# Second norm of a transformer layer: GpSimd's product moved to VectorE, and the order of the work around it

## The chip, the cores and the metric

The kernel runs on one core of a Trainium2 chip. The metric is the device time of one execution in microseconds (us), the median of several runs. The engines are TensorE (PE in the rows, with its weight loads as PEld), VectorE (DVE), ScalarE (ACT), GpSimd (POOL) and SyncE (SP), which issues most of the transfers.

## The reference, cut to what matters

One layer handles 512 prompt and 32 sample positions (544 columns) of 1024 features. All of it is fp32. The change lies between the layer's first residual sum and its FFN:

```
x  = x + gate1 * (merged @ w_out)
h2 = RMSNorm(x) * g_norm2 * (1 + scale2) + shift2      # RMSNorm: x * rsqrt(mean(x*x) + eps) over the features
up, gate = split(h2 @ w_up)
x  = x + gate2 * ((silu(dwconv3_causal(up)) * gate) @ w_down)
```

The scale, shift and gate come from a conditioning vector, one value for each feature and stream (prompt or sample). A final RMSNorm follows.

## The kernel before

Features lie on the 128 partitions (8 groups k = 0 to 7 of 128 features), positions on the free axis. The 544 columns are two halves of 272: 256 prompt and 16 sample columns each. Since scale and shift differ by stream, an operation that uses them is issued twice for a half, on 256 and on 16 columns (`streams`).

Every fp32 matrix product is made of three products of a high and a low part: `mm3_steps` issues for each k the matmuls (weight high, x high), (weight high, x low) and (weight low, x high), 272 columns each. So x must be split too: ScalarE writes the high part (a copy that rounds, L91), VectorE the low part (value less high part, L92).

Around the second norm the work stands as follows.

- `out_half(i)` computes the last four of eight output tiles of `merged @ w_out` (m = 4 to 7) for half i alone: 24 matmuls for each m. After each, `residual` adds the tile to x on VectorE (L676, one instruction for each stream), ScalarE squares the new row (L680), and GpSimd adds the squares of m = 1 to 6 into `sacc` (L682). The square of m = 7 stays apart in `sq2`.
- `norm(half)` sums the squares over the partitions with two matmuls against ones (L689, `ssh`; in the trace each has two records), and `rstd_of` makes `rs`, the reciprocal root, with ScalarE (L170, L172) and VectorE (L171, L174 to L176).
- `h2(half)` makes the normalised input for each k: GpSimd multiplies x by `rs` (L699, `hf`), VectorE applies scale and shift (L702, two instructions), then the split: high part by ScalarE (L91, `h2h`), low part by VectorE (L92, `h2l`).
- `up_half(half)` multiplies by the first three tiles of `w_up` (`first`: up tile 0, gate tile 0, up tile 1), whose weights are loaded and split ahead and which hold all three PSUM accumulators (`acc`).

The calls stand in this order: `out_half(0)`, `out_half(1)`, norm of half 0, `h2` of half 0, norm of half 1, `up_half(0)`, `h2` of half 1, `up_half(1)`. A scheduler then sets the order on each engine, and each engine executes its own list strictly in order. `after(inst, earlier)` tells that scheduler that `inst` stands behind `earlier`. Before, only the scale and shift instructions of k = 5 to 7 of half 0 are put behind the last residual sum of half 1 (`done`).

After `up_half(1)` come the other tiles of the FFN, each with a fresh accumulator. The next product (gate tile 1) takes the accumulator of up tile 0, once ScalarE has copied that tile out of PSUM (L752).

Of the kernel before, what the change touches and what calls it, by code (L numbers as in the profile page):

```python
# [12 lines left out]
F32 = mybir.dt.float32  # L13
F32R = mybir.dt.float32r
AF = mybir.ActivationFunctionType
ALU = mybir.AluOpType
# [34 lines left out]
def build(tc, a):  # L51
    nc = tc.nc
    ctx = ExitStack()
    with ctx:
# [34 lines left out]
        def split(hi, lo, x, eng=nc.vector):  # L89

            nc.scalar.copy(hi, x)  # L91
            eng.tensor_tensor(lo, x, hi.bitcast(F32), ALU.subtract)  # L92
# [10 lines left out]
        HALF = ((0, HT), (HT, T))  # L103

        def mm3_steps(ps, wh, wl, xh, xl, k0=0, nk=KD, first=True, last=True, cols=HALF):
            for k in range(nk):
                for w, xs in ((wh, (xh, xl)), (wl, (xh,))):
                    for n, x in enumerate(xs):
                        s = first and k == 0 and w is wh and n == 0
                        e = last and k == nk - 1 and w is wl  # L110
                        for i, (c0, c1) in enumerate(cols):
                            nc.tensor.matmul(ps[:, i, 0:c1 - c0], w[:, k], x[:, k0 + k, c0:c1], start=s, stop=e)  # L112
                yield

        def mm3(*args, **kw):
            for _ in mm3_steps(*args, **kw):
                pass
# [3 lines left out]
        def acc():  # L121
            acc_pools.rotate(-1)
            return acc_pools[-1].tile([P, 2, 512], F32, tag="mm", name="ps")[:, :, 0:HT]
# [30 lines left out]
        def after(inst, earlier):  # L154

            tc.add_manual_dep(inst.ins, earlier.ins.name,
                              mybir.DependencyInfo(mybir.DependencyClass.NoSync, mybir.DependencyReason.DATA))
# [27 lines left out]
        mods = cp.tile([P, 6, KD, 2], F32, name="mods")  # L185
# [144 lines left out]
        for k in range(KD):  # L330
# [5 lines left out]
            hf = xt[:, k]  # L336
# [4 lines left out]
        for w, slot, post in zip(ws, slots, (queries, keys)):  # L341
            ps = slot[:, :, 0:HT]
# [166 lines left out]
        earlier = None  # L509
        for j in range(NP):  # L510
            for e in range(2):
# [7 lines left out]
                earlier = (j, e, transposed(sg), vt)  # L519
# [112 lines left out]
        for b, w0, wb, br in ((0, 7 * KD, "w_branch_b", (bh, bl)), (1, 6 * KD, "w_branch_a", (oh, ol))):  # L632
# [7 lines left out]
            for m in range(KD):  # L640
                ps = proj(W[w0 + m], x)
                sg = mbp.tile([P, 2, HT], F32, tag="sg", bufs=2, name="sgm")
                last = nc.scalar.activation(sg, ps, AF.Sigmoid)
                ps = proj(load_w(a[wb][m], lo=nc.gpsimd), br)
# [15 lines left out]
        xr = xp.tile([P, KD, T], F32, name="xr")  # L660
# [3 lines left out]
        rs = xp.tile([P, T], F32, name="rs")  # L664
        sq2 = xp.tile([P, T], F32, name="sq2")

        def streams(c0, c1):

            e = c0 // HT * HT + HP
            return [(n, a_, b_) for n, a_, b_ in ((0, c0, min(c1, e)), (1, max(c0, e), c1)) if a_ < b_]  # L670

        def residual(ps, s, m, c0, c1):

            for n, a_, b_ in streams(c0, c1):
                r = xr[:, m, a_:b_]
                added = nc.vector.scalar_tensor_tensor(r, ps[:, a_ - c0:b_ - c0], mods[:, s, m, n:n + 1], r,  # L676
                                                       ALU.mult, ALU.add)
            sq = sacc[:, c0:c1] if m == 0 else sq2[:, c0:c1] if m == KD - 1 else \
                xp.tile([P, HT], F32, tag="sq", bufs=2, name="sq")
            nc.scalar.activation(sq, xr[:, m, c0:c1], AF.Square)  # L680
            if 0 < m < KD - 1:
                nc.gpsimd.tensor_tensor(sacc[:, c0:c1], sacc[:, c0:c1], sq, ALU.add)  # L682
            return added
# [8 lines left out]
        h2h = hp.tile([P, KD, T], F32R, tag="hh", name="h2h")  # L692
        h2l = hp.tile([P, KD, T], F32R, tag="hl", name="h2l")

        def h2(c0, c1, earlier=None):

            for k in range(KD):
                hf = xp.tile([P, HT], F32, tag="hf", bufs=6, name="hf2")
                nc.gpsimd.tensor_tensor(hf, xr[:, k, c0:c1], rs[:, c0:c1], ALU.mult)  # L699
                for n, a_, b_ in streams(c0, c1):  # L700
                    v = hf[:, a_ - c0:b_ - c0]
                    v = nc.vector.tensor_scalar(v, v, mods[:, 4, k, n:n + 1], mods[:, 3, k, n:n + 1], ALU.mult, ALU.add)  # L702
                    if earlier and k >= 5:
                        after(v, earlier)
                split(h2h[:, k, c0:c1], h2l[:, k, c0:c1], hf)

        tables = log_tables(last)
        wo = tc.alloc_tile_pool(name="wo", bufs=1)
# [1 line left out]
        for m in range(KD - NW):  # L710
            ps = proj(a["w_out"][m], (mh, ml))
# [2 lines left out]
        late = [(m, load_w(a["w_out"][m], pool=wo, hl_bufs=NW)) for m in range(KD - NW, KD)]  # L714

        def out_half(i):
            for m, w in late:
                ps = acc()[:, 0:1]
                mm3(ps, *w, mh, ml, cols=(HALF[i],))
                done = residual(ps[:, 0], 2, m, *HALF[i])  # L720
            return done

        def up_half(i):
            for w, ps in first.values():
                mm3(ps[:, i:i + 1], *w, h2h, h2l, cols=(HALF[i],))

        out_half(0)
        done = out_half(1)
# [3 lines left out]
        first = {m: (load_w(a["w_up"][m], pool=early, hl_bufs=3), acc()) for m in (0, KF, 1)}  # L732
# [14 lines left out]
        for f in range(KF):  # L747
            ps = first[f][1] if f in first else proj(a["w_up"][f], (h2h, h2l))
# [7 lines left out]
            ps = first[KF][1] if f == 0 else proj(a["w_up"][KF + f], (h2h, h2l))  # L756
# [7 lines left out]
        for m in range(KD - 1):  # L764
            ps = acc()
# [8 lines left out]
        m = KD - 1  # L774
# [7 lines left out]
        for c in HALF:  # L782
            ps = acc()[:, 0:1]
# [3 lines left out]
            cs = slice(*c)  # L787
# [74 lines left out]
```

## Time and profile before

| What | Value |
|---|---|
| Median of 3 runs | 1077.73 us (1075.47 to 1080.16) |
| Profiled execution, its own time | 1078.02 us |
| Span of that execution, first to last instruction | 1075.9 us |
| Busy in the span: TensorE | 1035.5 us (96%) |
| VectorE | 616.3 us (57%) |
| ScalarE | 390.1 us (36%) |
| GpSimd | 159.6 us (15%) |
| Mean granted TensorE clock, as a share of full speed | 0.987 |

The shares are averages over the whole span. The 2.1 us between span and time lie outside the instructions.

### The profile page before, as it was taken

How to read it: one execution, taken by the hardware profiler on the slowest of the kernel's cores; microseconds unless marked ns; L12 is line 12 of the kernel's file. 1: busy time of each engine (PE TensorE's matmuls, PEld its weight loads, DVE VectorE, ACT ScalarE, POOL GpSimd, SP SyncE). 2: the span in 40 equal slices, each digit the busy share in tenths (PEclk: the TensorE clock that was granted, in tenths of full speed). 3: DMA queues.
4: the chain of work that ended last, by engine and by line, in shares of the span. 5: the costliest groups of instructions: out<-in, count | busy, mean ns of one | idle time of the engine just before them, and what ended most of it. 6: DMA issues, size and time to landing. Idle time of an engine off the chain costs nothing.

```text
span 1075.9 us, 19430 instructions
## 1 busy us (share of the span) xinstructions
PE 1035.5 (96%) x8106; PEld 1017.2 (95%) x8106; DVE 616.3 (57%) x930; ACT 390.1 (36%) x655; POOL 159.6 (15%) x245
## 2 busy tenths in 40 slices
PE   2899999999999999999999999999999999999995
PEld 1689999999999999999999999999999999999995
DVE  6956666565675557566667568545455544422234
ACT  5455555444443332121222343333233323322231
POOL 2410010000001111211121135000010001000112
PEclk9799999999999999999999999999999999999998
DMA  9636555454212224555545650022322232332312
GB/s 374 236 88 199 140 143 145 142 140 129 80 50 89 95 83 141 175 179 173 187 166 177 213 203 1 22 98 79 99 79 98 79 98 80 91 87 76 90 53 83
DMA packets 43272, 133.45 MB, mean 124 GB/s; under 512 B 5296, under 2 KB 8496, under 8 KB 43056
## 3 DMA queue, kind: packets, MB, share of 16 engines
q1 hardware_dynamic: 43040, 132.07, 38.5%
q8 instruction: 63, 1.03, 0.4%
q14 instruction: 25, 0.20, 0.1%
q10 hardware_dynamic: 144, 0.14, 0.1%
HBM read 112.60 MB, written 6.75 MB: 111 GB/s over the span
## 4 chain that ended last, share of the span: by engine, by line
PE 92%; DVE 4%; issue 1%; DMA 1%; ACT 1%; POOL 0%; SPq 0%; DVEq 0%; POOLq 0%; ACTq 0%
PE ps L112 83%; PE z L371 2%; PE o L371 2%; PE at L413 2%; DVE hf L702 1%; PE slot L112 1%; PE mt L315 1%; DVE adum L196 1%; DMA cbc<-in_c_dram 1%; DVE h2l L92 1%; DVE xt L337 0%; PE so L371 0%; PE tp L268 0%; SPq L289 0%; POOL hl L92 0%
## 5 line engine op out<-in xcount | busy, mean ns | idle before, releaser
L99 ACT CAST wh<-raw 128x1024 fp32r<-128x1024 f32 x153 | 159.1, 1040 | 362.2 <-PE ps L112 264.3
L100 DVE TENSOR_TENSOR wl<-raw,wh 128x1024 fp32r<-128x1024 f32 (+1 forms) x133 | 162.1, 1221 | 190.2 <-ACT wh L99 189.6
L112 PE MATMUL ps<-hh,wh 128*128 128x272 f32 x992 | 209.3, 291 | 0.0
L112 PE MATMUL ps<-hh,wl 128*128 128x272 f32 x992 | 205.2, 288 | 0.0
L112 PE MATMUL ps<-hl,wh 128*128 128x272 f32 x992 | 204.9, 288 | 0.0
L112 PEld LDWEIGHTS ps<-hh,wh 128*128 128x128 f32 x992 | 156.0, 188 | 1.6 <-issue 0.5
L112 PEld LDWEIGHTS ps<-hl,wh 128*128 128x128 f32 x992 | 155.7, 188 | 0.0
L112 PEld LDWEIGHTS ps<-hh,wl 128*128 128x128 f32 x992 | 155.1, 189 | 0.0
L112 PE MATMUL ps<-h2l,wh 128*128 128x272 f32 x704 | 150.1, 289 | 1.1 <-DVE h2l L92 1.0
L112 PE MATMUL ps<-h2h,wl 128*128 128x272 f32 x704 | 150.6, 290 | 0.0
L112 PE MATMUL ps<-h2h,wh 128*128 128x272 f32 x704 | 150.1, 289 | 0.3 <-ACT h2h L91 0.3
L112 PEld LDWEIGHTS ps<-h2l,wh 128*128 128x128 f32 x704 | 112.7, 189 | 2.0 <-DVE h2l L92 1.9
L112 PEld LDWEIGHTS ps<-h2h,wh 128*128 128x128 f32 x704 | 112.8, 189 | 0.9 <-ACT h2h L91 0.8
L112 PEld LDWEIGHTS ps<-h2h,wl 128*128 128x128 f32 x704 | 112.1, 190 | 0.0
L196 DVE SCALAR_TENSOR_TENSOR adum<-araw,cbc 128x1024 f32<-128x1024 f32 x64 | 81.3, 1270 | 44.8 <-DMA araw<-in_w_ada_dram 44.1
L100 POOL TENSOR_TENSOR wl<-raw,wh 128x1024 fp32r<-128x1024 f32 x20 | 50.0, 2500 | 170.8 <-ACT wh L99 151.5
L112 PE MATMUL ps<-fh,wh 128*128 128x272 f32 x308 | 63.6, 288 | 0.0
L112 PE MATMUL ps<-fl,wh 128*128 128x272 f32 x308 | 63.5, 288 | 0.0
L112 PE MATMUL ps<-fh,wl 128*128 128x272 f32 x308 | 63.4, 287 | 0.0
L398 DVE TENSOR_TENSOR_SCAN keep<-keep,zero 128x512 f32<-128x512 f32 (+1 forms) x64 | 47.7, 805 | 20.1 <-ACT keep L397 20.1
L112 PEld LDWEIGHTS ps<-fl,wh 128*128 128x128 f32 x308 | 48.3, 188 | 0.0
L112 PEld LDWEIGHTS ps<-fh,wh 128*128 128x128 f32 x308 | 48.2, 189 | 0.0
(201 smaller groups left out, 1544.3 us busy)
## 6 DMA issues: line engine op xcount, KB each, us to landing
raw<-in_w_in_dram SPq DMA_DIRECT2D x64, 512.0 KB, 3.6
raw<-in_w_up_dram SPq DMA_DIRECT2D x44, 512.0 KB, 3.5
araw<-in_w_ada_dram SPq DMA_DIRECT2D x32, 512.0 KB, 4.2
kt<-ko SPq DMA_DIRECT2D x32, 256.0 KB, 5.2
raw<-in_w_down_dram SPq DMA_DIRECT2D x16, 512.0 KB, 3.5
mraw<-in_w_ada_dram SPq DMA_DIRECT2D x10, 512.0 KB, 7.1
qt<-qo SPq DMA_DIRECT2D x32, 136.0 KB, 2.5
raw<-in_w_branch_b_dram SPq DMA_DIRECT2D x8, 512.0 KB, 3.5
```

The costliest lines, as they stand in the source:

```text
L92: eng.tensor_tensor(lo, x, hi.bitcast(F32), ALU.subtract)
L99: nc.scalar.copy(wh[:, :nk], raw[:, :nk])
L100: lo.tensor_tensor(wl[:, :nk], raw[:, :nk], wh[:, :nk].bitcast(F32), ALU.subtract)
L112: nc.tensor.matmul(ps[:, i, 0:c1 - c0], w[:, k], x[:, k0 + k, c0:c1], start=s, stop=e)
L196: nc.vector.scalar_tensor_tensor(adum, raw, 1.0, cbc[:, n], ALU.mult, ALU.mult, accum_out=sums[:, n:n + 1])
L315: nc.tensor.matmul(rows, sct[:, i], raw[:, i * P:i * P + P], start=i == 0, stop=i == KD - 1, skip_group_check=True)
L371: nc.tensor.matmul(out, l, r, start=s, stop=t, skip_group_check=True)
L398: nc.vector.tensor_tensor_scan(kb, kb, zero.broadcast_to([P, w]), 1.0, ALU.mult, ALU.add)
L413: nc.tensor.transpose(at[:, c + P * b:c + P * b + P], sg[:, s0:s0 + P], ident)
L702: v = nc.vector.tensor_scalar(v, v, mods[:, 4, k, n:n + 1], mods[:, 3, k, n:n + 1], ALU.mult, ALU.add)
```

## The change

`h2` no longer uses GpSimd. For each k and stream VectorE computes (x * scale) * `rs` in one instruction with two tensor inputs (SCALAR_TENSOR_TENSOR); ScalarE then writes the high part as Identity with the shift as bias, and VectorE the low part as (value + shift) - high. The split is now made by stream too. `out_half` returns its last three residual sums (m = 5, 6, 7), and `h2` of half 0 puts its prompt products of k >= 1 behind the sum of m = 5, of k >= 3 behind m = 6, and of k >= 5 behind m = 7. `up_half` takes the three tiles in turn for each k.

```
-        def h2(c0, c1, earlier=None):
+        def h2(c0, c1, earlier=()):
 
             for k in range(KD):
                 hf = xp.tile([P, HT], F32, tag="hf", bufs=6, name="hf2")
-                nc.gpsimd.tensor_tensor(hf, xr[:, k, c0:c1], rs[:, c0:c1], ALU.mult)
                 for n, a_, b_ in streams(c0, c1):
+                    cs = slice(a_, b_)
                     v = hf[:, a_ - c0:b_ - c0]
-                    v = nc.vector.tensor_scalar(v, v, mods[:, 4, k, n:n + 1], mods[:, 3, k, n:n + 1], ALU.mult, ALU.add)
-                    if earlier and k >= 5:
-                        after(v, earlier)
-                split(h2h[:, k, c0:c1], h2l[:, k, c0:c1], hf)
+                    i = nc.vector.scalar_tensor_tensor(v, xr[:, k, cs], mods[:, 4, k, n:n + 1], rs[:, cs], ALU.mult, ALU.mult)
+                    for first_k, add in zip((1, 3, 5), earlier):
+                        if k >= first_k and n == 0:
+                            after(i, add)
+                for n, a_, b_ in streams(c0, c1):
+                    cs = slice(a_, b_)
+                    v, shift = hf[:, a_ - c0:b_ - c0], mods[:, 3, k, n:n + 1]
+                    nc.scalar.activation(h2h[:, k, cs], v, AF.Identity, bias=shift)
+                    nc.vector.scalar_tensor_tensor(h2l[:, k, cs], v, shift, h2h[:, k, cs].bitcast(F32), ALU.add, ALU.subtract)
...
         def out_half(i):
+            done = []
             for m, w in late:
                 ps = acc()[:, 0:1]
                 mm3(ps, *w, mh, ml, cols=(HALF[i],))
-                done = residual(ps[:, 0], 2, m, *HALF[i])
-            return done
+                done.append(residual(ps[:, 0], 2, m, *HALF[i]))
+            return done[1:]
 
         def up_half(i):
-            for w, ps in first.values():
-                mm3(ps[:, i:i + 1], *w, h2h, h2l, cols=(HALF[i],))
+
+            for _ in zip(*[mm3_steps(ps[:, i:i + 1], *w, h2h, h2l, cols=(HALF[i],)) for w, ps in first.values()]):
+                pass
```

VectorE's list before, around the residual sums of m = 6 (`ps_7197`) and m = 7 (`ps_7227`) of half 1; `hf2_7284` and `hf2_7290` are the buffers of k = 3 and 4 of half 0, `hf2_7296` that of k = 5:

```order
L702 TENSOR_SCALAR hf2_7284<-hf2_7284,mods_83 128x256
L702 TENSOR_SCALAR hf2_7284<-hf2_7284,mods_83 128x16
L702 TENSOR_SCALAR hf2_7290<-hf2_7290,mods_83 128x256
L92 TENSOR_TENSOR h2l_6734<-hf2_7278,h2h_6733 128x272
L92 TENSOR_TENSOR h2l_6734<-hf2_7284,h2h_6733 128x272
L702 TENSOR_SCALAR hf2_7290<-hf2_7290,mods_83 128x16
L676 SCALAR_TENSOR_TENSOR xr_6721<-ps_7197,mods_83,xr_6721 128x256
L676 SCALAR_TENSOR_TENSOR xr_6721<-ps_7197,mods_83,xr_6721 128x16
L92 TENSOR_TENSOR h2l_6734<-hf2_7290,h2h_6733 128x272
L676 SCALAR_TENSOR_TENSOR xr_6721<-ps_7227,mods_83,xr_6721 128x256
L676 SCALAR_TENSOR_TENSOR xr_6721<-ps_7227,mods_83,xr_6721 128x16
L702 TENSOR_SCALAR hf2_7296<-hf2_7296,mods_83 128x256
```

The same list after the change, between the same two sums; k = 3, 4 and 5 are `hf2_7287`, `hf2_7294` and `hf2_7301`:

```order
L676 SCALAR_TENSOR_TENSOR xr_6721<-ps_7197,mods_83,xr_6721 128x16
L702 SCALAR_TENSOR_TENSOR hf2_7287<-xr_6721,mods_83,rs_6731 128x256
L702 SCALAR_TENSOR_TENSOR hf2_7294<-xr_6721,mods_83,rs_6731 128x256
L702 SCALAR_TENSOR_TENSOR hf2_7294<-xr_6721,mods_83,rs_6731 128x16
L702 SCALAR_TENSOR_TENSOR hf2_7301<-xr_6721,mods_83,rs_6731 128x16
L710 SCALAR_TENSOR_TENSOR h2l_6734<-hf2_7287,mods_83,h2h_6733 128x256
L710 SCALAR_TENSOR_TENSOR h2l_6734<-hf2_7294,mods_83,h2h_6733 128x256
L710 SCALAR_TENSOR_TENSOR h2l_6734<-hf2_7294,mods_83,h2h_6733 128x16
L710 SCALAR_TENSOR_TENSOR h2l_6734<-hf2_7301,mods_83,h2h_6733 128x16
L676 SCALAR_TENSOR_TENSOR xr_6721<-ps_7227,mods_83,xr_6721 128x256
L676 SCALAR_TENSOR_TENSOR xr_6721<-ps_7227,mods_83,xr_6721 128x16
```

Before, the instructions of k = 0 to 4 were spread over the sums; after it, the prompt products of k = 3 and 4 stand between the sums of m = 6 and m = 7, and those of k = 5 to 7 behind the latter.

TensorE's list before, from the seventh matmul with half 0 of `h2h` and `h2l` on; `ps_7320` is up tile 0, `ssh` the sum of squares of half 1:

```order
L112 MATMUL ps_7320<-h2h_6733,wh_7316 128x272
L112 MATMUL ps_7320<-h2l_6734,wh_7316 128x272
L112 MATMUL ps_7320<-h2h_6733,wl_7317 128x272
L112 MATMUL ps_7320<-h2h_6733,wh_7316 128x272
L112 MATMUL ps_7320<-h2l_6734,wh_7316 128x272
L689 MATMUL ssh_7335<-sq2_6732,ones_69 128x272
L689 MATMUL ssh_7335<-sacc_6730,ones_69 128x272
L112 MATMUL ps_7320<-h2h_6733,wl_7317 128x272
```

After the change, from the fourth such matmul on, with up tile 0 as `ps_7328`, gate tile 0 as `ps_7335` and up tile 1 as `ps_7342`:

```order
L112 MATMUL ps_7335<-h2h_6733,wh_7331 128x272
L112 MATMUL ps_7335<-h2l_6734,wh_7331 128x272
L112 MATMUL ps_7335<-h2h_6733,wl_7332 128x272
L112 MATMUL ps_7328<-h2h_6733,wh_7324 128x272
L112 MATMUL ps_7342<-h2h_6733,wh_7338 128x272
L112 MATMUL ps_7342<-h2l_6734,wh_7338 128x272
L112 MATMUL ps_7342<-h2h_6733,wl_7339 128x272
L112 MATMUL ps_7328<-h2l_6734,wh_7324 128x272
L689 MATMUL ssh_7343<-sq2_6732,ones_69 128x272
L689 MATMUL ssh_7343<-sacc_6730,ones_69 128x272
L112 MATMUL ps_7328<-h2h_6733,wl_7325 128x272
```

In both, 11 matmuls stand ahead of `ssh`. Before, they use k = 0 to 3 of one tile; after it, k = 0 of three tiles and the start of k = 1. The count of matmuls does not change: 144 with `h2` in the two halves of the three tiles.

## Rows read from the trace of the kernel before

**Rows 1.** Timeline of TensorE (start us, duration us, instruction, idle before).

```profile
646.46 0.68 PE L689 MATMUL ssh<-sq,ones 128*128 128x272 f32 x2
647.56 0.29 PE L112 MATMUL ps<-mh,wh 128*128 128x272 f32 x1
...
658.07 0.29 PE L112 MATMUL ps<-mh,wl 128*128 128x272 f32 x1
658.19 0.29 PE L112 MATMUL ps<-h2h,wh 128*128 128x272 f32 x1
...
661.76 0.73 PE L689 MATMUL ssh<-sq,ones 128*128 128x272 f32 x2 [1.77 <-ACT sq L680]
...
677.75 0.29 PE L112 MATMUL ps<-h2h,wl 128*128 128x272 f32 x1
...
683.93 0.42 PE L112 MATMUL ps<-h2h,wh 128*128 128x272 f32 x2
```

**Rows 2.** Busy time by stretch; PEclk is the granted clock, 1.00 is 2.4 GHz.

```profile
core 0: us, PE busy (x) PEld busy (x) DVE busy (x) ACT busy (x) POOL busy (x), PEclk, DMA share, GB/s
661.75:663.20 1.45, 1.44 (x6) 1.21 (x7) 1.45 (x7) 0.84 (x2) 0.15 (x1) 0.79 0.02 6
663.20:666.10 2.90, 2.90 (x15) 2.90 (x15) 2.56 (x8) 1.23 (x3) 0.21 (x1) 0.52 0.00 0
672.80:677.80 5.00, 3.57 (x19) 2.42 (x18) 4.57 (x15) 2.09 (x5) 0.00 (x0) 1.00 0.00 0
677.00:1054.00 377.00, 377.00 (x3010) 376.90 (x3010) 160.68 (x224) 118.69 (x174) 36.70 (x98) 1.00 0.26 81
```

**Rows 3.** The chain that ended last, in order of time (start us, us, what).

```profile
660.71 0.54 DVE xr L676 x2
...
677.00 377.41 PE ps L112 x3011
```

**Rows 4.** Timeline of VectorE, ScalarE and GpSimd around the sums.

```profile
645.27 0.63 DVE L676 SCALAR_TENSOR_TENSOR xr<-ps,mods,xr 128x256 f32<-128x256 f32 x2 [2.38 <-PE ps L112]
645.93 0.43 ACT L680 ACTIVATE sq<-xr 128x272 f32<-128x272 f32 x1 [2.52 <-DVE xr L676]
...
660.62 0.62 DVE L676 SCALAR_TENSOR_TENSOR xr<-ps,mods,xr 128x256 f32<-128x256 f32 x2
660.92 0.76 POOL L682 TENSOR_TENSOR sacc<-sacc,sq 128x272 f32<-128x272 f32 x1 [2.45 <-ACT sq L680]
661.16 1.74 DVE L702 TENSOR_SCALAR hf<-hf,mods 128x256 f32<-128x256 f32 x5
...
665.37 0.45 DVE L176 SCALAR_TENSOR_TENSOR rs<-nt,rs 128x272 f32<-128x272 f32 x1
...
678.08 0.68 ACT L752 COPY up<-ps 128x512 f32<-128x512 f32 x2 [1.08 <-PE ps L112]
```

**Rows 5.** VectorE by line and shape, 666.5 to 672.6 us: GpSimd works beside it.

```profile
L702 DVE TENSOR_SCALAR hf<-hf,mods 128x256 f32<-128x256 f32 x4 | 3.7, 913 | 0.9 <-POOL hf L699 0.9
L702 DVE TENSOR_SCALAR hf<-hf,mods 128x16 f32<-128x16 f32 x3 | 2.2, 742 | 0.0
```

**Rows 6.** The same, 672.6 to 677 us: GpSimd is idle.

```profile
L702 DVE TENSOR_SCALAR hf<-hf,mods 128x256 f32<-128x256 f32 x5 | 2.5, 509 | 0.0
L92 DVE TENSOR_TENSOR h2l<-hf,h2h 128x272 fp32r<-128x272 f32 x5 | 2.0, 434 | 0.0
L702 DVE TENSOR_SCALAR hf<-hf,mods 128x16 f32<-128x16 f32 x5 | 1.4, 285 | 0.0
```

**Rows 7.** Groups of ScalarE and VectorE by shape, over the span (mean ns behind the busy us).

```profile
L339 ACT ACTIVATE xt<-xt,mods 128x512 f32<-128x512 f32 x8 | 6.5, 815 | 0.9 <-DVE xt L337 0.5
L339 ACT ACTIVATE xt<-xt,mods 128x32 f32<-128x32 f32 x8 | 3.2, 399 | 0.0
...
L466 DVE SCALAR_TENSOR_TENSOR fcv<-up,vec,fcv 128x546 f32<-128x546 f32 x44 | 34.7, 789 | 3.0
L464 DVE TENSOR_SCALAR fcv<-up,vec 128x546 f32<-128x546 f32 x22 | 12.3, 559 | 1.3 <-ACT up L752 1.3
```

## The prediction, made before the changed kernel ran

> **What bounds the kernel now.** I read the chain of waits first. From 677.00 us on it is 377.41 us of TensorE alone [rows 3], and in 677 to 1054 us TensorE is busy in all 377.00 us at the full granted clock [rows 2]. So whatever moves the start of that stretch moves the end of the kernel by as much. Ahead of it the chain runs through VectorE: residual sums of `xr` and what stands around them [rows 3]. The timeline of TensorE then shows what that costs [rows 1]. The products with `h2h` begin at 658.19 us, and the next tile of the FFN (gate tile 1, behind the 144 matmuls of the two `up_half`) at 683.93 us: 25.74 us. The reader is to compare this with the work in it. 377.00 us hold 3010 matmuls [rows 2], 0.125 us each, so 144 take 18.0 us. The sum of squares cost 647.56 - 646.46 = 1.10 us with one ordinary matmul in it [rows 1], so about 1.0 us for itself. Work is 19.0 us, and 6.7 us are lost. Three places show most of it:
>
> - 1.77 us of idle before the sum of squares of half 1, released by a square of ScalarE [rows 1].
> - Behind that idle the granted clock is 0.79 and then 0.52, the 1.2 GHz level, until 666.10 us [rows 2]. In 661.75 to 666.10 us (4.35 us) I count 14 ordinary matmuls beside the sum of squares, 2.75 us of work at full clock: 1.6 us lost.
> - In 672.80 to 677.80 us TensorE holds 19 matmuls, at 0.125 us 2.4 us of work in 5.00 us [rows 2]: 2.6 us lost, in pauses for `h2h` and `h2l` of half 1. The clock stays 1.00 there although TensorE is busy in only 3.57 us of the 5.00.
>
> That makes 6.0 us; the other 0.7 us are pauses too short to sort.
>
> **The change, step by step.**
>
> *Sums first.* TensorE ends m = 7 of half 1 at 658.07 + 0.29 = 658.36 us [rows 1], but VectorE adds it only at 660.62 us [rows 4], 2.3 us late, behind work for `h2`. In the new order the add follows a block of eight instructions (two 256-wide and two 16-wide products, and as many low parts). A 256-wide and a 16-wide instruction of the same kind as the new ones took 0.54 us as a pair [rows 3], so the block is 4 pairs, 2.2 us, and with the add of m = 6 ahead of it 2.7 us. The tiles end 24 x 0.125 = 3.0 us apart, so VectorE is about free at 658.4 us. After an undelayed add the square started 645.93 - 645.27 = 0.66 us and the sum of squares 646.46 - 645.27 = 1.19 us later [rows 1, 4]. That gives 658.4 + 1.2 = 659.6 us. TensorE gets there 11 matmuls after 658.19 us, at 659.57 us: no wait. The block also waits once for ScalarE, which I take as 0.3 us; I use 0.3 us of remaining wait, from bounds of 0 and 0.8 us (one GpSimd add, 0.76 us [rows 4], in full).
>
> *The norm of half 1.* Before, `rs` was complete at 665.37 + 0.45 = 665.82 us, 4.06 us after its sum of squares began at 661.76 us [rows 1, 4]. From 659.6 us on this gives 663.7 us, and 664.0 us with the 0.3.
>
> *`h2` of half 1.* VectorE now has two pairs for each k, 1.08 us [rows 3]. The trace has no product of two SBUF tensors in this shape, so its bounds are the nearest rows: below, the low part of 272 columns, 434 ns, for each pair [rows 6], 0.87 us for a k; above, the scale and shift instructions while GpSimd worked, 913 + 742 ns a pair [rows 5], 3.3 us for a k. I take 1.08: it is a row of the same kind of instruction, and GpSimd has nothing left to do there. How much GpSimd matters is seen in the old 256-wide instruction: 913 ns beside it, 509 ns without [rows 5, 6]. ScalarE has two instructions for each k; with scale and bias it took 815 ns for 512 and 399 ns for 32 columns [rows 7], so at most 1.2 us, and it runs beside VectorE. Eight k then take 8.6 us at VectorE's price: from 664.0 to 672.6 us, with 0.5 us for the last low part 673.1 us. TensorE, now in turn over three tiles, takes 9 matmuls or 1.13 us for each k. Half 0 keeps it busy until 658.19 + 9.0 + 1.0 + 0.3 = 668.5 us, and it wants k = 7 of half 1 at 676.4 us. There are 3 us in hand. Taken tile by tile, as before, it would want k = 7 at 668.5 + 7 x 0.38 = 671.1 us and wait 2 us: the order by feature carries the second saving.
>
> *What falls away.* Without 1.77 us of idle I expect no fall of the clock; pauses like those at 672.80 to 677.80 us left it at 1.00 [rows 2]. GpSimd's 16 products cost nothing, since they were off TensorE, but their time beside VectorE goes.
>
> *What is late next.* The three tiles now end together, and gate tile 1 needs the accumulator of up tile 0. Before, that tile ended 6 us ahead of the need: its last matmul ended at 677.75 + 0.29 = 678.04 us, ScalarE's copies ran from 678.08 to 678.76 us [rows 1, 4], and TensorE had two tiles left to do. Now the last matmul of up tile 0 starts 7 matmuls (0.88 us) before TensorE would go on, ends 0.59 us before, and the copies end 0.04 + 0.68 us later, 0.13 us too late. With a release I take 0.2 us. The accumulators of gate tile 0 and up tile 1 are wanted 6 us (48 matmuls) and 12 us later. Between the first copy and the release of the first of them lie 559 + 2 x 789 ns of VectorE [rows 7] and some four steps of that size, an estimate of 5 us: hidden behind gate tile 1.
>
> **A rule against it.** A single-input instruction of 546 columns took 559 ns and a two-input one 789 ns [rows 7]. The Trainium skill, "VectorE: DVE Perf Modes", section "The perf-mode tier table", says why: fp32 with one SBUF source gets two elements a cycle, `tensor_tensor` one. By that the new products are dearer for each element than the scale and shift they replace, and VectorE would end with more work than it had undisturbed. By the rows, undisturbed, a k cost 509 + 285 + 434 = 1.23 us of durations before [rows 6] against 1.08 us of start-to-start now; both stay far below what TensorE can wait for, so the sum is the same by either.
>
> **The sum.** Lost before 6.7 us; left 0.3 us before the sum of squares and 0.2 us at the accumulator. Gain 6.2 us (0.58%). Against the profiled execution, 1078.02 us: 1071.8. That execution lies 0.3 us above the median of 1077.73, so the median should come to about 1071.5; I say 1071.6.
>
> **The rivals.**
>
> *The wait stays at the sums.* The add of m = 7 comes late again, because the block before it is slower than 2.2 us. For it: five instructions of the old kind took 1.74 us partly beside a GpSimd add [rows 4], hardly slowed, but steady GpSimd work nearly doubled them [rows 5, 6], and the add of squares of m = 6 falls into this block. The Trainium skill, "SBUF — State Buffer", section "Who interferes with whom", says that a VectorE instruction with two SBUF inputs and a GpSimd one that reads SBUF lock each other out for a whole instruction; 660.92 us shows no such block, 666.5 to 672.6 us fits one. Worked out from rows: if the add is 1.8 us late, TensorE idles 1.8 us, the clock falls as before (1.6 us), and the gain is 6.7 - 0.2 - 3.4 = 3.1 us: 1074.6. It decides from a block of about 4 us. One GpSimd add alone reaches 0.8 us.
>
> *No change.* The saved time is eaten behind 677 us, by weights or by VectorE. Against it: TensorE is never idle there and VectorE is busy in 160.68 us of 377 [rows 2]. Time 1077.5.
>
> *Slower.* VectorE becomes the bound of half 1. If a pair costs what it did beside GpSimd, 1.66 us, a k takes 3.3 us, k = 7 is ready at 664.0 + 26.5 + 0.5 = 691.0 us, TensorE goes on 1.1 + 0.2 us later, at 692.3 us instead of 683.93: 8.4 us slower, 1086. It decides from 2.2 us a k, where 664.0 + 8 x 2.2 + 1.8 us reaches 683.4. Against it: no GpSimd work is left there.
>
> **How the numbers follow.** The forecast has 0.64 (1070 to 1073.5), the sums' wait 0.24 (1073.5 to 1077), no change 0.07, slower 0.05. Runs of one kernel spread from 1075.47 to 1080.16 us, so about 0.5% (5.4 us) is what a measurement tells from nothing. A gain of 6.2 us lies little above it: of the forecast's chance I put 0.54 above, of the second case 0.03. Faster 0.57, same 0.38, slower 0.05. The range goes from 1069.8 (the full 6.5 us, and a median 1.4 us lower by spread) to 1076.0, most of the second case.
>
> **What would show it.** Right: the sum of squares of half 1 starts near 659.6 us with under 0.5 us of idle; granted clock 1.00 throughout; no pauses for `h2h` or `h2l` from 668 to 677 us; gate tile 1 starts near 677.7 us, with a pause of about 0.2 us released by ScalarE's copy. Wrong: the add of m = 7 later than 659.5 us; a clock of 0.5 after it; a pair of new products above 0.75 us start to start; a pause longer than 1 us at the accumulator.

## The result, and the profile of the changed kernel

| | Median | Runs (lowest to highest) |
|---|---|---|
| Kernel before, same chip | 1078.17 us | 5 (1075.47 to 1080.16) |
| Kernel after | 1071.99 us | 5 (1070.02 to 1072.90) |
| Ratio | 0.9947 | 95% interval 0.9934 to 0.9960 |

The medians lie 6.2 us apart, and the forecast was 6.2 us. That they agree to a tenth is luck: the interval of the ratio allows 4.3 to 7.1 us. The profiled executions (1078.02 and 1070.02 us) lie 8.0 us apart, because the one of after had come to the first product with `h2h` 2.5 us earlier, at 655.70 against 658.19 us [rows 1]. That start wanders from run to run (655.35 to 659.72 us in the kernels below), so from here on I compare one **stretch**: from TensorE's first matmul with `h2h` to its first matmul of gate tile 1. Before it took 25.74 us, and the work in it is 19.0 us. After it the two kernels are alike: 1075.9 - 683.93 = 391.97 us and 1067.6 - 675.50 = 392.10 us to the end of the span.

Busy time by stretch of the kernel after, columns as in rows 2: the stretch, and what follows it.

```profile
655.70:675.50 19.80, 19.39 (x151) 18.82 (x149) 14.60 (x52) 9.54 (x28) 0.37 (x3) 1.00 0.00 1
675.50:1046.00 370.50, 370.50 (x2959) 370.50 (x2960) 159.98 (x223) 117.96 (x172) 37.62 (x98) 1.00 0.26 82
```

The stretch is 19.80 us, 5.94 us shorter, at a granted clock of 1.00 throughout. GpSimd is busy for 0.37 us of it. The end is still set by TensorE alone. The timeline of TensorE shows the only two pauses left:

```profile
655.70 0.29 PE L112 MATMUL ps<-h2h,wh 128*128 128x272 f32 x1
...
657.13 0.36 PE L112 MATMUL ps<-h2h,wh 128*128 128x272 f32 x1 [0.40 <-DVE xr L676]
657.70 0.62 PE L689 MATMUL ssh<-sq,ones 128*128 128x272 f32 x2
...
675.20 0.29 PE L112 MATMUL ps<-h2h,wl 128*128 128x272 f32 x1
675.50 0.52 PE L112 MATMUL ps<-h2h,wh 128*128 128x272 f32 x2
```

The sum of squares (L689) no longer waits; before it had 1.77 us of idle. The 0.40 us stand at the seventh matmul, the first of up tile 1, which needs the accumulator that the sum of m = 7 sets free. Gate tile 1 starts 0.30 us after the matmul ahead of it, 0.17 us more than a matmul's 0.125; ScalarE's copies of up tile 0 end at 675.45 us, 0.05 us before that start. The other 0.2 us above the work of 19.0 us are too short to sort. The chain that ended last passes from VectorE to TensorE's long stretch behind the residual sum of m = 7; before, it passed only at 677.00 us [rows 3]:

```profile
656.45 0.55 DVE xr L676 x2
657.13 0.73 PE ps L112 x4
657.87 0.92 PE ssh L689 x4
658.78 16.70 PE ps L112 x133
675.50 370.59 PE ps L112 x2958
```

The timeline of VectorE around the sums of m = 6 and m = 7, which answers to rows 4:

```profile
653.12 0.62 DVE L676 SCALAR_TENSOR_TENSOR xr<-ps,mods,xr 128x256 f32<-128x256 f32 x2
653.66 1.71 DVE L702 SCALAR_TENSOR_TENSOR hf<-xr,mods,rs 128x256 f32<-128x256 f32 x4
655.29 1.16 DVE L710 SCALAR_TENSOR_TENSOR h2l<-hf,mods,h2h 128x256 fp32r<-128x256 f32 x4
656.37 0.62 DVE L676 SCALAR_TENSOR_TENSOR xr<-ps,mods,xr 128x256 f32<-128x256 f32 x2
```

The tile of m = 7 ends at 655.86 us (a last matmul at 655.57 of 0.29 us). Its add starts 0.51 us later; before, it was 2.3 us. Between the two adds lies the block of eight instructions, 656.37 - 653.66 = 2.71 us. VectorE by line and shape in half 1 of `h2` (661.3 to 671.5 us), to be held against rows 5 and 6:

```profile
L702 DVE SCALAR_TENSOR_TENSOR hf<-xr,mods,rs 128x256 f32<-128x256 f32 x8 | 3.8, 477 | 0.0
L710 DVE SCALAR_TENSOR_TENSOR h2l<-hf,mods,h2h 128x256 fp32r<-128x256 f32 x8 | 3.8, 477 | 0.3 <-ACT h2h L709 0.3
L702 DVE SCALAR_TENSOR_TENSOR hf<-xr,mods,rs 128x16 f32<-128x16 f32 x8 | 1.8, 226 | 0.0
L710 DVE SCALAR_TENSOR_TENSOR h2l<-hf,mods,h2h 128x16 fp32r<-128x16 f32 x8 | 1.8, 226 | 0.0
```

All four kinds have one price from the first k to the last. Before, a kind had two: 913 and 742 ns beside GpSimd [rows 5], and without it 285 ns for 16 columns and, for 256 columns, not the 509 ns of rows 6 but 403. The mean of 509 holds one instruction of 0.93 us that began beside GpSimd's last product, at 671.86 us. The kernel before, in 672.8 to 677 us (first row), and over half 0 of `h2` (648 to 664 us), where GpSimd works beside part of it:

```profile
L702 DVE TENSOR_SCALAR hf<-hf,mods 128x256 f32<-128x256 f32 x4 | 1.6, 403 | 0.0
...
L702 DVE TENSOR_SCALAR hf<-hf,mods 128x256 f32<-128x256 f32 x8 | 5.5, 686 | 0.7 <-POOL hf L699 0.7
L702 DVE TENSOR_SCALAR hf<-hf,mods 128x16 f32<-128x16 f32 x8 | 3.6, 454 | 0.0
```

### The profile page after: what moved, and what is told of

Same layout as the page of the kernel before. It is cut to its first block, busy times and chain, and to the rows that moved or that the text cites. A ratio compares the mean times of both kernels' runs of the same rounds, so it can differ in the third digit from the quotient of the medians.

```text
span 1067.6 us, 19434 instructions
## 1 busy us (share of the span) xinstructions
PE 1030.8 (97%) x8106; PEld 1014.3 (95%) x8106; DVE 613.4 (57%) x946; ACT 394.4 (37%) x671; POOL 149.0 (14%) x229
## 4 chain that ended last, share of the span: by engine, by line
PE 92%; DVE 4%; issue 1%; DMA 1%; ACT 0%; SPq 0%; POOL 0%; DVEq 0%; ACTq 0%; POOLq 0%
PE ps L112 84%; PE z L371 3%; PE o L371 2%; DVE adum L196 2%; PE at L413 2%; DMA cbc<-in_c_dram 1%; PE slot L112 0%; DVE xt L337 0%; PE ssh L689 0%; PE so L371 0%; SPq L289 0%; PE tp L268 0%; DVE hf L702 0%; DVE h2l L710 0%; POOL hl L92 0%
## 5 line engine op out<-in xcount | busy, mean ns | idle before, releaser
L682 POOL TENSOR_TENSOR sacc<-sacc,sq 128x272 f32<-128x272 f32 x24 | 27.3, 1154 | 151.5 <-ACT sq L680 151.5
```

## The experiments

The forecast came true, but that alone doesn't show that its reasons did. Two views were to be told apart. The prediction's own: the **orders** bring the gain, the sums first in half 0, the order by feature in half 1. The rival: it is **GpSimd's product**, through its time beside VectorE and through the waits for its result. The change has three parts, so each was run alone and each was left out. All kernels, the stretch from the profiled execution of each (after and e11, which differ in idle memsets far ahead of the stretch, show how close two of them come):

| Kernel | Stretch (us) | Median (us) | Before, same chip | Ratio, 95% interval |
|---|---|---|---|---|
| before | 25.74 | | | |
| after | 19.80 | 1071.99 | 1078.17 | 0.9947 (0.9934 to 0.9960) |
| e1 new `h2` only | 19.75 | 1070.55 | 1077.06 | 0.9948 (0.9931 to 0.9966) |
| e2 sums first only | 28.59 | 1081.51 | 1077.06 | 1.0043 (1.0027 to 1.0060) |
| e3 by feature only | 23.14 | 1075.19 | 1077.06 | 0.9981 (0.9968 to 0.9994) |
| e4 both orders, old `h2` | 26.51 | 1078.37 | 1077.06 | 1.0009 (0.9997 to 1.0021) |
| e5 after, old place of sums | 19.54 | 1070.86 | 1076.77 | 0.9938 (0.9918 to 0.9959) |
| e6 after, old `up_half` | 19.86 | 1070.08 | 1076.77 | 0.9936 (0.9917 to 0.9955) |
| e7 after, tiles staggered | 19.50 | 1070.66 | 1076.77 | 0.9935 (0.9918 to 0.9952) |
| e8 after, idle GpSimd products, half 1 | 24.99 | 1076.49 | 1076.77 | 0.9995 (0.9983 to 1.0006) |
| e9 before, product on VectorE | 20.26 | 1071.28 | 1077.98 | 0.9928 (0.9910 to 0.9946) |
| e10 after, idle GpSimd products, half 0 | 30.17 | 1081.38 | 1077.98 | 1.0032 (1.0019 to 1.0044) |
| e11 after, GpSimd memsets | 19.78 | 1070.58 | 1077.98 | 0.9918 (0.9897 to 0.9939) |
| e12 after, strictly tile by tile | 21.41 | 1072.71 | 1077.98 | 0.9943 (0.9920 to 0.9965) |

The letters A, B and C in the expectations stand for views as each of them words it.

**e1: the new `h2` alone.** The kernel after with both orders taken back:

```diff
-                    for first_k, add in zip((1, 3, 5), earlier):
-                        if k >= first_k and n == 0:
-                            after(i, add)
+                    if earlier and k >= 5:
+                        after(i, earlier[-1])
...
-            for _ in zip(*[mm3_steps(ps[:, i:i + 1], *w, h2h, h2l, cols=(HALF[i],)) for w, ps in first.values()]):
-                pass
+            for w, ps in first.values():
+                mm3(ps[:, i:i + 1], *w, h2h, h2l, cols=(HALF[i],))
```

> Only the new arithmetic of h2 (GpSimd's product on VectorE); sums and tiles ordered as before. The measure is the stretch from TensorE's first matmul with h2h to the first of gate tile 1: 25.74 us before, 19.80 us with the whole change, 19.0 us of work. Theory A, each wait has its own cure: the sums come on time because VectorE's work ahead of them is shorter, so the idle of 1.77 us and the fall of the clock go; but tile by tile TensorE wants k = 7 of half 1 some 2 us before VectorE has it, so pauses of about 2 us stay: stretch 21.5 us, some 4 us faster than before. Theory B, GpSimd beside VectorE was the whole cost: stretch about 20 us. Theory C, only the order counts: stretch 24 us or more, clock falls.

The stretch is 19.75 us, the sum of squares stands 1.54 us behind the first matmul without a wait, and no pause is left. This one part gives the whole gain, though not on TensorE's old order: the list under e6 shows what the scheduler makes of it.

**e2: sums first alone**, on the old `h2` (and `out_half` returns the list of sums):

```diff
-                    if earlier and k >= 5:
-                        after(v, earlier)
+                    for first_k, add in zip((1, 3, 5), earlier):
+                        if k >= first_k and n == 0:
+                            after(v, add)
```

> Only the order of the sums (products of k >= 1, 3, 5 behind the sums of m = 5, 6, 7); GpSimd keeps its products, tiles one by one. Theory A: the sum of squares starts about 1.4 us after the first matmul with h2h, without a fall of the clock, but k = 5 to 7 of half 0 now come late for the first tile (1.5 to 2 us) and half 1 still pauses (about 3 us): stretch 23.5 to 24.5 us, 1 to 2 us faster than before. Theory B: no gain, 25.5 us. Theory C: the first wait is gone for good, 22 us.

It is slower than before. The timeline of VectorE shows what stands ahead of the sums of m = 6 and m = 7 (start, duration, instruction, idle before):

```profile
660.62 0.29 DVE L702 TENSOR_SCALAR hf<-hf,mods 128x16 f32<-128x16 f32 x1 [0.66 <-POOL hf L699]
660.83 0.62 DVE L676 SCALAR_TENSOR_TENSOR xr<-ps,mods,xr 128x256 f32<-128x256 f32 x2
661.36 0.72 DVE L702 TENSOR_SCALAR hf<-hf,mods 128x256 f32<-128x256 f32 x2
662.31 1.21 DVE L92 TENSOR_TENSOR h2l<-hf,h2h 128x272 fp32r<-128x272 f32 x2 [0.22 <-ACT h2h L91]
663.45 0.61 DVE L676 SCALAR_TENSOR_TENSOR xr<-ps,mods,xr 128x256 f32<-128x256 f32 x2
```

The tile of m = 7 ends at 658.83 us (its last matmul starts at 658.54 and takes 0.29); its add comes at 663.45, 4.6 us late. Only the prompt products were put behind the sums; the 16-column ones of a later k stand ahead of them, and wait 0.66 us for GpSimd's product with the sums queued behind. TensorE pauses 1.77, 0.45 and 0.76 us ahead of the sum of squares, and the granted clock is 0.50 from 663.67 to 668.67 us. What the rule moves is only as good as the instructions that it leaves in front.

**e3: by feature alone** (the old kernel with the new `up_half`).

> Only the tiles feature by feature; GpSimd keeps its products, sums late as before. Theory A: the pauses of half 1 vanish (2.6 us), the idle before the sum of squares and the fall of the clock stay, and the idle moves to the seventh matmul, since up tile 1 waits for the accumulator that the late sum of m = 7 frees: idle about 2.3 us, clock 0.5 behind it, stretch about 23.3 us. Theory B: no gain, 25.5 us.

No pause in half 1, but 1.68 and 0.25 us in half 0, both released by a residual sum (DVE xr L676): three tiles want three accumulators within a few matmuls, and the sums of m = 6 and 7 hold two of them. Stretch 23.14 us, granted clock 0.74 from 660.76 to 665.76 us. The gain of about 2 us is a third of the whole by the medians.

**e4: both orders, the old `h2`** (the edits of e2 and e3 together).

> Both orders, but h2 as before, with GpSimd's products. Theory A: sums on time, and TensorE's nine matmuls for each k give VectorE and GpSimd time enough: the last low part of half 1 is ready about 17.4 us after the first matmul with h2h, wanted at 18.5; stretch about 19.9 us, the same time as the whole change. Theory B: GpSimd's neighbourhood is what cost: 23 us or more. Theory C: 19.8 us.

The timeline of TensorE, its waits in half 0:

```profile
659.20 0.36 PE L112 MATMUL ps<-h2h,wh 128*128 128x272 f32 x1 [2.21 <-DVE xr L676]
661.81 0.56 PE L112 MATMUL ps<-h2h,wh 128*128 128x272 f32 x1 [1.88 <-DVE xr L676]
```

Late sums (e2) and the early need for their accumulators (e3) meet. Both orders together, without the new arithmetic, give nothing. This is the run that fells the prediction's attribution.

**e5 and e6: the kernel after without one order each.** e5 has the first half of e1's edit, e6 the second.

> The change without its order of the sums: new h2 and tiles feature by feature, the old rule (only k >= 5 behind the last sum). Theory A: VectorE's work ahead of the sum of m = 7 is short enough without the rule, so the stretch stays 19.8 to 20.3 us. The forecast's step, that the new order of the sums removes the first wait, would want the idle and the fall of the clock back: 22 to 23.5 us.

> The change without the tiles feature by feature. Theory A: the first tile wants k = 7 of half 0 about 3.6 us after its first matmul, VectorE has it at about 4.9 us, since it now stands behind the sums: 1.4 us of pauses there; in half 1 about 1 us more: stretch 21.5 us. The forecast says only the pauses of half 1 return, about 2 us: 21.8 us. If feature by feature is worth nothing: 19.8 us.

Neither order is missed: 19.54 and 19.86 us. In e6 I had counted on a wait for k = 7 of half 1. There is none, and the order of TensorE's instructions says why: the scheduler doesn't keep to the tiles as the code has them. Matmuls of half 1 before, in e6 and in e9 (below), in runs of one tile (t0 is up tile 0, g0 gate tile 0, t1 up tile 1):

```
before: t0 x24; g0 x24; t1 x24
e6: t0 x16; g0 x2; t0 x2; g0 x1; t0 x1; g0 x4; t0 x2; g0 x3; t0 x1; g0 x2; t0 x2; g0 x12; t1 x24
e9: t0 x10; g0 x1; t0 x5; g0 x5; t0 x1; g0 x4; t0 x2; g0 x6; t0 x1; g0 x2; t0 x3; g0 x1; t0 x2; g0 x5; t1 x24
```

From k = 5 on it slips matmuls of the second tile between those of the first. It does by itself, for two tiles, what the new `up_half` writes out. It does so in e1, e6 and e9, where the product has left GpSimd, and not before or in e2; why is not shown. So e1, e6 and e9 take away GpSimd's product and change TensorE's order at once, and only e12 holds that order.

**e12: tile by tile in earnest.** e6, with the first matmul of each tile put behind the last of the tile ahead:

```diff
+            last = None
             for w, ps in first.values():
-                mm3(ps[:, i:i + 1], *w, h2h, h2l, cols=(HALF[i],))
+                tile = list(mm3_steps(ps[:, i:i + 1], *w, h2h, h2l, cols=(HALF[i],)))
+                if last:
+                    after(tile[0][0], last)
+                last = tile[-1][-1]
```

> The kernel after with the old order of the two up_half, and TensorE held to it: the first matmul of each tile is put behind the last of the tile ahead (in e6 the scheduler itself moved matmuls of the second tile between those of the first). Theory A (the prediction's: tile by tile TensorE wants k = 7 of half 1 about 2 us before it is there): sum of squares of half 1 within 0.5 us as in e6, then pauses of 1 to 2 us together for h2h and h2l of half 1 (k = 5 to 7), stretch 20.8 to 22 us, ratio 0.995 to 0.997. Theory B (half 1 is ready in time whatever the order): no pause, stretch 19.9 us, ratio 0.9936.

The timeline of TensorE at k = 7 of half 1 (the first three rows are k = 6, the other two k = 7):

```profile
669.38 0.28 PE L113 MATMUL ps<-h2h,wh 128*128 128x272 f32 x1
669.66 0.39 PE L113 MATMUL ps<-h2l,wh 128*128 128x272 f32 x1
669.89 0.29 PE L113 MATMUL ps<-h2h,wl 128*128 128x272 f32 x1
670.26 0.39 PE L113 MATMUL ps<-h2h,wh 128*128 128x272 f32 x1
670.72 0.40 PE L113 MATMUL ps<-h2l,wh 128*128 128x272 f32 x1
```

At one matmul for each 0.125 us the first four gaps between starts hold 0.15, 0.10, 0.25 and 0.34 us of waiting, 0.8 us in half 1 where the prediction had 2; half 0 waits 0.6 us at one place and 0.2 us at another. The stretch is 1.55 us longer than e6's. So with TensorE strictly tile by tile, as it was before in half 1, 4.3 us of the 5.9 us are gained (21.41 against 25.74 us); the other 1.6 us need an order that crosses the tiles, written out or found by the scheduler. The medians of e12 and after can't be told apart.

**e7: the tiles staggered**, the kernel after with another order in `up_half` (half 0 two tiles in turn and then the third, half 1 in turn for five k and then tile by tile):

```diff
+            g = [mm3_steps(ps[:, i:i + 1], *w, h2h, h2l, cols=(HALF[i],)) for w, ps in first.values()]
+            order = (KD * (0, 1) + KD * (2,)) if i == 0 else (5 * (0, 1, 2) + 3 * (0,) + 3 * (1,) + 3 * (2,))
+            for t in order:
+                next(g[t])
```

> The change with another turn of the three tiles: in half 0 up tile 0 and gate tile 0 in turn and up tile 1 after them; in half 1 all three in turn for k = 0 to 4, then each tile's last three k. If the pause of 0.4 us at the seventh matmul is the accumulator that the sum of m = 7 frees, and the one at gate tile 1 the accumulator of up tile 0, both go: stretch 19.1 us, the time about 0.7 us below the changed kernel's, less than the runs can tell. If the pause of 0.4 us is a low part or high part that comes late, it stays: 19.6 us.

Both pauses of the kernel after are gone (the accumulators are wanted later and come free earlier), 0.26 us stay at the sum of squares. 19.50 us against 19.80: a difference that the trace shows and that the runs are too wide to measure.

**e8: GpSimd put back, with nobody waiting for it.** The kernel after, with 16 products in half 1 that no instruction reads:

```diff
+        idle = xp.tile([P, HT], F32, name="idle")
...
+                for _ in range(2 if c0 else 0):
+                    nc.gpsimd.tensor_tensor(idle, xr[:, k, c0:c1], rs[:, c0:c1], ALU.mult)
```

> The change with 16 more GpSimd products beside h2 of half 1, two for each k, of the same operands as the removed ones, into a tile that nobody reads. Tests what GpSimd's neighbourhood costs the new two-input instructions. If they block each other: a pair takes 0.85 us or more start to start, k = 7 of half 1 comes about 20.5 us after the first matmul with h2h, wanted at 18.5: pauses of 1 to 3 us, stretch 21 to 23 us. If they do not: pairs stay at 0.54 us, stretch 19.8 us.

VectorE by line and shape while they run (661.3 to 675.9 us; its L706 and L714 are L702 and L710 of after), and GpSimd:

```profile
L706 DVE SCALAR_TENSOR_TENSOR hf<-xr,mods,rs 128x256 f32<-128x256 f32 x7 | 6.1, 869 | 0.0
L714 DVE SCALAR_TENSOR_TENSOR h2l<-hf,mods,h2h 128x256 fp32r<-128x256 f32 x5 | 4.5, 908 | 0.0
L714 DVE SCALAR_TENSOR_TENSOR h2l<-hf,mods,h2h 128x16 fp32r<-128x16 f32 x5 | 3.7, 732 | 0.0
L706 DVE SCALAR_TENSOR_TENSOR hf<-xr,mods,rs 128x16 f32<-128x16 f32 x6 | 2.4, 398 | 0.0
...
L702 POOL TENSOR_TENSOR idle<-xr,rs 128x272 f32<-128x272 f32 x16 | 13.5, 843 | 6.5 <-DVE rs L176 5.3
```

Against the rows of after, the same instructions take 1.8 to 3.2 times as long, although VectorE waits for no result of GpSimd's here, and although the lists of TensorE, VectorE and ScalarE are those of after, instruction for instruction. TensorE pauses three times for `h2l`, 1.27, 1.28 and 1.26 us, the stretch is 5.2 us longer, and the ratio is 0.9995: time beside VectorE alone eats nearly all of the gain. (16 products here, 8 for a half in the kernel before.)

Single instructions show what is added. Two of VectorE's (start, duration), each with the product of GpSimd's that ran when it started:

```profile
665.43 1.00 DVE L714 SCALAR_TENSOR_TENSOR h2l<-hf,mods,h2h 128x256 fp32r<-128x256 f32 x1
665.15 1.00 POOL L702 TENSOR_TENSOR idle<-xr,rs 128x272 f32<-128x272 f32 x1
666.36 0.74 DVE L714 SCALAR_TENSOR_TENSOR h2l<-hf,mods,h2h 128x16 fp32r<-128x16 f32 x1
666.23 0.84 POOL L702 TENSOR_TENSOR idle<-xr,rs 128x272 f32<-128x272 f32 x1
```

The 256 columns end 0.28 us after the product, the 16 columns 0.03 us after it. It is the same for all 16 slowed instructions of that window, nine of 256 and seven of 16 columns; the others took their usual 0.47 and 0.22 us. So an instruction here either runs at its usual rate or first waits for the end of the product.

**e10: the same beside half 0** (`range(0 if c0 else 2)`).

> The kernel after, with 16 GpSimd products that nobody reads beside h2 of half 0 (e8 had them beside half 1). Theory A (order decides; the add of m = 7 stands early in VectorE's list): the add stays within 0.5 us of its tile, stretch 19.8 us, ratio as for the kernel after, 0.995. Theory B (locks): a pair of VectorE takes about 1.2 to 1.4 us instead of 0.54, the block of 4 pairs between the sums of m = 6 and m = 7 about 5 us instead of 2.7, so the add comes 2 to 3 us late in spite of its early place, TensorE waits about as long for the accumulator or the sum of squares, and the clock falls behind it: stretch 22 to 24.5 us, ratio 0.997 to 0.9995.

The timeline of VectorE between the sums of m = 6 and m = 7, the place shown above for after:

```profile
659.44 0.61 DVE L676 SCALAR_TENSOR_TENSOR xr<-ps,mods,xr 128x256 f32<-128x256 f32 x2
659.98 2.21 DVE L706 SCALAR_TENSOR_TENSOR hf<-xr,mods,rs 128x256 f32<-128x256 f32 x4
662.12 3.27 DVE L714 SCALAR_TENSOR_TENSOR h2l<-hf,mods,h2h 128x256 fp32r<-128x256 f32 x4
665.31 0.61 DVE L676 SCALAR_TENSOR_TENSOR xr<-ps,mods,xr 128x256 f32<-128x256 f32 x2
```

and of TensorE:

```profile
660.20 0.36 PE L112 MATMUL ps<-h2h,wh 128*128 128x272 f32 x1 [2.58 <-DVE xr L676]
666.07 0.57 PE L112 MATMUL ps<-h2h,wh 128*128 128x272 f32 x1 [5.13 <-DVE xr L676]
```

The lists of TensorE, VectorE and ScalarE are again those of after, with the sum of m = 7 at its early place. The block ahead of it takes 5.33 us instead of 2.71, and TensorE waits 7.7 us in all. My own upper figure for the stretch, 24.5 us, was far too low: it had one block growing, but blocks stand ahead of the sums of m = 5 and m = 6 too. Counted from the first matmul with `h2h` (657.09 us here), the sums of m = 5, 6 and 7 come 2.3, 4.9 and 7.5 us later than in after, and the clock falls behind the waits. GpSimd's own add of the square of m = 6 is late too, since it stands behind the idle products, but TensorE does not wait for it: both waits end with a residual sum. An early place in the list is worth nothing while the instructions ahead of it take twice their time.

**e9: one word.** The kernel before, its rules of order and its arithmetic kept:

```diff
-                nc.gpsimd.tensor_tensor(hf, xr[:, k, c0:c1], rs[:, c0:c1], ALU.mult)
+                nc.vector.tensor_tensor(hf, xr[:, k, c0:c1], rs[:, c0:c1], ALU.mult)
```

> The kernel before with one word changed: the product of x and rs runs on VectorE instead of GpSimd; scale and shift, split and both orders stay as they were. VectorE has one more instruction of 272 columns for each k, so by work alone it is worse off: 0.44 us for the product (the row of L175, a product of two SBUF tensors of 272 columns, 0.44 us), 0.51 and 0.29 us for scale and shift, 0.43 us for the low part, 1.67 us of durations for a k against 1.23 us. Theory A (what VectorE has to do counts, and the gain comes from the shorter arithmetic): the sums come late as before or later, half 1 has pauses, stretch 25.7 us or more, ratio 1.000 or above. Theory B (GpSimd beside VectorE is the cost, in its locks and as a late input): rows of L702 fall to about 0.51 us in both halves, the add of m = 7 comes within 1 us of its tile, no 1.77 us of idle and no fall of the clock; in half 1 eight k take about 12 us against 8.6, so up to 2 us of pauses stay: stretch 20 to 22.5 us, ratio 0.995 to 0.9975.

VectorE by line and shape, 650 to 676 us, both halves:

```profile
L702 DVE TENSOR_SCALAR hf<-hf,mods 128x256 f32<-128x256 f32 x16 | 7.0, 438 | 0.0
L92 DVE TENSOR_TENSOR h2l<-hf,h2h 128x272 fp32r<-128x272 f32 x16 | 6.6, 435 | 0.1
L699 DVE TENSOR_TENSOR hf<-xr,rs 128x272 f32<-128x272 f32 x16 | 6.5, 434 | 0.0
L702 DVE TENSOR_SCALAR hf<-hf,mods 128x16 f32<-128x16 f32 x16 | 5.1, 317 | 0.0
```

VectorE has one instruction more for each k than before (438 + 435 + 434 + 317 = 1.62 us of durations), and the stretch is 20.26 us with one pause of 0.61 us. The ratio, 0.9928, is as good as that of after. The sum of m = 7 did not move forward in VectorE's list: ahead of it stand the same fifteen instructions of scale, shift and low part as before, and seven products besides. From `rs` to that sum the 22 take 8.9 us where the fifteen took 10.3. TensorE's list of half 1 did change (under e6). Against e1, which has the same rules, the shorter arithmetic is worth 0.5 us of the stretch; the rest is that the product left GpSimd, with the order that the scheduler then finds.

**e11: GpSimd that only writes** (e8's instructions replaced by memsets of 544 columns).

> As e8, but the 16 idle GpSimd instructions only write (a memset of 544 columns each) and read nothing. Theory A (any GpSimd work that touches SBUF beside VectorE's two-input instructions slows them): L702 and L710 as long beside it as in e8, 0.87 and 0.91 us for 256 columns, and pauses in half 1 for as long as the memsets last; stretch above 21 us. Theory B (it is GpSimd's reading that shuts out VectorE's second input): L702 and L710 stay at 0.48 us, 0.54 us a pair, no pause; stretch 19.5 to 20.0 us, ratio 0.9945.

It missed its place. A memset waits for nothing, so all 16 had ended at 618.55 us, more than 31 us ahead of `h2` of half 0, beside other work of VectorE, and the run says nothing of half 1. What it does show is that other work:

```profile
608.83 9.72 POOL L702 MEMSET idle<- 128x544 f32 x16 [8.24 <-PE ps L112]
...
609.64 0.72 DVE L649 TENSOR_TENSOR mb<-mb,sgm 128x544 f32<-128x544 f32 x1
610.28 1.22 DVE L100 TENSOR_TENSOR wl<-raw,wh 128x1024 fp32r<-128x1024 f32 x1
611.41 0.72 DVE L92 TENSOR_TENSOR ml<-mb,mh 128x544 fp32r<-128x544 f32 x1
```

These three have two SBUF inputs each, and in the kernel after, with GpSimd idle, they take 0.73, 1.22 and 0.72 us. The memsets cost them nothing.

## Why the prediction was right, and where its reasons were not

The time, the sum and most of its terms held; what failed is the cause to which the two largest terms were given. The stretch became 5.94 us shorter where 6.2 us were forecast.

- **What bounds the kernel.** Right: 370.50 us of TensorE alone at the end, and whatever the stretch lost came back in the time.
- ***Sums first*.** The term came true (the 1.77 us of idle and the fall of the clock are gone), its cause did not. The step says that the add is on time because it follows a block of eight instructions in the new order. With the old place of the sums the stretch is the same (e5), with the new place and the old `h2` it is longer than before (e2). The block itself was put at 2.2 us and took 2.71; the remaining 0.3 us of wait came as 0.40 us at an accumulator, a wait that I had not named and that e3, e4 and e10 show in full.
- ***The norm of half 1*.** Forecast 664.0 - 658.19 = 5.8 us behind the first matmul with `h2h`; measured 661.47 - 655.70 = 5.77 us.
- ***`h2` of half 1*.** 8.6 + 0.5 us forecast from `rs` to the last low part, 670.65 - 661.51 = 9.14 us measured. The price of the pair was right. "The order by feature carries the second saving" was not: e6 without it has no wait in half 1, since I had read the order of TensorE off the code and not off its list of instructions. Held strictly tile by tile (e12), half 1 loses 0.8 us and not 2, and the whole stretch 1.55 us.
- ***What falls away*.** The step that failed. "GpSimd's 16 products cost nothing, since they were off TensorE, but their time beside VectorE goes" named the cause in half a sentence and gave it no price. It had one in rows 5 and 6: 913 against 403 ns and 742 against 285 ns in half 1. In half 0 the means of eight were 686 and 454 ns. That is what made the sums late in half 0 and `h2` late in half 1, the two losses that I divided between the orders. e8 and e10 show, with all other lists unchanged, that neighbourhood alone costs 5.2 and 10.4 us of the stretch; e9 shows that taking it away gives the gain without any other edit, and e12 that 4.3 us of it do not hang on an order that crosses the tiles. On VectorE the slower instructions were the larger part of the loss before: in half 1 they add 4 x (913 - 403) + 3 x (742 - 285) ns = 3.4 us, in half 0, by the means of eight, 3.6 us, against one wait for GpSimd's result of 0.9 us [rows 5] and one of 0.7. How much of TensorE's loss each brought no run separates: e9 removes both.
- ***What is late next*.** 0.2 us at gate tile 1 forecast, 0.17 measured.
- **The rule on perf modes.** The sum did not need it, but the rows bear it out. With GpSimd idle the old scale and shift takes 403 ns for 256 columns and 285 for 16, the new product 477 and 226: the 240 columns between cost 0.12 and 0.25 us, half the price with one SBUF input, which agrees with the rule. The comparison beside it in the prediction was wrong: it set durations (1.23 us for a k, with the 509 in it) against start-to-start times (1.08). Durations on both sides are 403 + 285 + 434 ns = 1.12 us before and 2 x (477 + 226) ns = 1.41 us now. VectorE did get more work than it had undisturbed, and the kernel is faster all the same.
- **The rivals.** *The wait stays at the sums* was drawn with the right mechanism and a point of decision, a block of about 4 us. e10, at 5.33 us, is this rival made to happen, and dearer than the 3.4 us that I gave it (1.8 of idle, 1.6 of the clock), since three blocks grow and, in the order by feature, the late sums hold accumulators too. That the five instructions of 1.74 us were "hardly slowed" was a reading of a merged row: the first of them, beside the GpSimd add, took 0.70 us, the other two of 256 columns 0.40. *Slower* was to decide from 2.2 us a k in half 1. e8 has about that (661.2 to 678.9 us, 17.7 us for eight k) and comes out nearly level with before, as that point says.

The total could be right with a wrong cause because a faster VectorE removes the same two waits that were credited to the orders: both accounts come to the same sum. For the cause, then, the hit was luck.

The lock that the rival cited, the Trainium skill, "SBUF — State Buffer", section "Who interferes with whom" (a VectorE instruction with two SBUF inputs and a GpSimd one that reads SBUF shut each other out, one that only writes does not, and neither does a VectorE instruction with at most one SBUF input outside the two-port modes), agrees with all of this: 869 and 908 ns against 477 in e8; 0.72 and 1.22 us unchanged beside memsets in e11; and the residual sums, which take one input from PSUM, 0.47 us for 256 columns beside a GpSimd product (653.54 us in e10) and 477 ns in the kernel after. The prediction laid the two-input clause over 666.5 to 672.6 us, where the slowed scale and shift has one SBUF input. The same section has another clause for that: an instruction in a two-port mode, which it lets `tensor_scalar` enter, is shut out too. 913 against 403 ns and the half price of a column fit it. No run here shows two-port modes beside a writing GpSimd.

## What to carry to other kernels

An engine that is off the critical path can still be the reason for a wait on it: compare the duration of the same instruction with its neighbour busy and idle, and price the difference before crediting an order. Before writing an order out by hand, read the order that the engines really get, and try the removal alone. A total that comes true doesn't prove its parts: leave each part out once.

## What the runs showed of the hardware that was not expected

- Short instructions pay like long ones. Beside GpSimd's products a low part of 16 columns took 732 ns instead of 226 (0.51 us more), one of 256 columns 908 instead of 477 (0.43 us more): what is added is a wait for the end of the product, not a slower rate (e8, single instructions). GpSimd itself suffers little: 843 ns for a product in e8, up to 1.00 us at most, against 0.77 us for the one at 665.89 us in the kernel before, which ran while VectorE stood idle.
- The clock: three pauses of 1.26 to 1.28 us in 7 us left it at 1.00 (e8), one of 1.68 us in e3 was followed by a mean of 0.74 (660.76 to 665.76 us), and 2.58 and 5.13 us in e10 by 0.50 for the next 5.4 us.
